# A hybrid decoder trunk on one core: the mixers' normalized input written over X, retention tables loaded once or a stage ahead, retention gates fetched ahead of the state updates

## The chip, the core and the metric

The kernel runs on one core of one Trainium2 chip. The core has TensorE (PE, with its weight loads PEld), VectorE (DVE), ScalarE (ACT), GpSimd (POOL) and SyncE (SP), each with an instruction queue of its own that it works through in order. The metric is the device time of one execution in microseconds, lower being better.

## The reference, cut to what matters

One step of a two-layer trunk over 256 prompt positions and 8 sequences of 8 sampled positions (320 columns in all). In each layer three branches read the same normalized `h`:

```python
x = x + 0.5 * swiglu_ffn(rmsnorm(x, ffn1_norm), ...)
h = rmsnorm(x, mix_norm)
q, k, v, g_ret, u, z, xbc, dt_raw, gate_logits = split(h @ w_in)
y_ret, s_ret = retention_branch(q, k, v, g_ret, ...)   # rotary; scores * decay; state update; silu(g) * groupnorm(o)
y_s5,  s_s5  = s5_branch(u, ...)
y_ssd, s_ssm = ssd_branch(z, xbc, dt_raw, ...)
x = x + (gates[0]*y_ret + gates[1]*y_s5 + gates[2]*y_ssd) @ w_out
x = x + 0.5 * swiglu_ffn(rmsnorm(x, ffn2_norm), ...)
```

In the retention branch each of the four heads multiplies its scores by a decay table of its own and the sampled queries by `q_dec`, updates its state, normalizes its output over the head and multiplies it by the gate `silu(g)`.

## The kernel before, in words

**Layout.** Activations lie transposed, 128 channels by 320 columns; X is eight such tiles. Every matrix product is made of fp32r parts: a value is split into a high half (ScalarE copy, L304) and a low half (VectorE subtraction, L305), and `proj` (L287) multiplies each 128x128 weight block three times (L294 high by high, L295 high weight by low input, L296 low weight by high input). `stream` (L267) loads 512 KB of weights at a time with SP and splits them (L280 on ScalarE, L281 on VectorE); there are three raw, two high and two low buffers. One such chunk feeds 24 matmuls, one `proj` over eight input tiles.

**The pool `t`.** All 128x320 tiles of activations and tables come from one pool of 53 (`NT`). A tile's slot is taken by the first instruction that writes it.

**Order.** The program text is not the order of the engines. `weave` (L381) deals steps of side work (state-space groups, S5 blocks, retention heads) between the units of a main list; a planner then fixes, before the run and with its own costs, the order of the instructions on each engine's queue. Slots of one pool are handed out in program order with few exceptions, so the planner places an instruction that takes a `t` tile behind the first writers of the `t` tiles asked for before it.

**Start of the mixers** (L1338 to L1359). `scaled` splits X times the norm's gain before the norm's factor r is known, and the first seven projections run on these pairs: dt (L434), three of u and three of xBC; r is multiplied in afterwards, at L436 (dt, into a new `t` tile), L1204 (u, into a new `t` tile) and L517 and L518 (xBC). `ssd_dt` first asks for a table (`resets`, L431). In `norm` (L372) each X[k] is multiplied by gain and r into a new tile h (L377) and split. All later projections read these pairs. X itself was stored to DRAM (`xd`, L418) in the FFN before and comes back only for the residual after the mixers (L1427).

**Retention.** `ret_tabs` (L790) loads the two rotary tables. Each head (`ret_head`, L864, twelve steps) issues on GpSimd the loads of its state s0 (2 x 512 KB, L870) and of two tables, its mask `mk` and `qd` (L871, issued at L208). Two steps later the scores are multiplied by the mask (L882 to L884) and the sampled queries by `qd` (L886). Keys are transposed, scaled (L894), split (L573, L574) and spread by matmuls (L583). Outputs o are made (L914 to L921), the prompt state (L928 to L931) and the eight sampled states (L936, L938) are updated and stored (L940), and then the two gate tiles are fetched from DRAM (L943, issued at L1319). There follow mean and variance (L946 to L950, the Newton steps of `rstd_of` at L338 to L347, PE's broadcast L350, ScalarE's copy L353), the product of gate, gain and o (L953), the product with r (L954) and the split. The gates were made by `ret_gate` (L958) and stored to `sd` (L967).

The heads run in two weaves (L1397, L1398), two heads in each, beside gate projections and S5 blocks. Ahead of them a weave (L1387) ends with the eight units of the last state-space projection, `o`. After the heads the first product that needs all of them is `ret_w_o` (L1406).

Of the kernel before, what the change touches and what calls it, by code (L numbers as in the profile page):

```python
# [13 lines left out]
ALU = mybir.AluOpType  # L14
# [34 lines left out]
S5P = ((0,), (1, 2), (3, 4), (5, 6), (7,))  # L49
# [106 lines left out]
class Trunk:  # L156
# [139 lines left out]
            nc.tensor.matmul(p[:, :T], wl, xh, start=False, stop=k == n - 1)  # L296
        return p

    def split(self, src, hi=None):

        nc = self.nc
        hi = self.t(F32R)
        lo = self.t(F32R)
        nc.scalar.activation(hi, src, AF.Copy)  # L304
        nc.vector.tensor_tensor(lo, src, hi.bitcast(F32), op=ALU.subtract)  # L305
        return hi, lo
# [65 lines left out]
    def norm(self, l, name, r):  # L372
        nc = self.nc
        hs = []
        for k in range(KD):
            h = self.t()
            nc.vector.scalar_tensor_tensor(h, self.X[k], self.col(l, name, k), r, op0=ALU.mult, op1=ALU.mult)  # L377
            hs.append(self.split(h))
        return hs

# [409 lines left out]
    def ret_tabs(self):  # L790
        self.rot = self.tab(0), self.tab(1)

    def ret_qk(self, l, h, rot):

        nc = self.nc
        sts = {}

        def unit(nme, hd):
            if nme not in sts:
                sts[nme] = self.stream(f"w_{nme}", l)  # L800
            cos, sin = self.rot
            p = self.proj(sts[nme], h())
            sw = self.t()
            o = self.t()
            with self.soon():
                nc.scalar.activation(sw[0:64], p[64:128, :T], AF.Copy)
                nc.scalar.activation(sw[64:128], p[0:64, :T], AF.Copy)
                nc.vector.tensor_tensor(o, p[:, :T], cos, op=ALU.mult)
            nc.vector.tensor_tensor(sw, sw, sin, op=ALU.mult)
            nc.vector.tensor_tensor(o, o, sw, op=ALU.add)  # L810
            rot[nme, hd] = o

        return [lambda n=n, hd=hd: unit(n, hd) for n in "qk" for hd in range(RH)]
# [50 lines left out]
    def ret_head(self, l, hd, rot, v, vs, sd, out):  # L864
        nc, C, ap = self.nc, self.C, self.ap
        V, S = nc.vector, nc.scalar
        kd = C["kdec"].rearrange("p (b h) -> p b h", b=3)
        s0 = [self.A(4, 256) for _ in range(2)]
        for i in range(2):
            nc.gpsimd.dma_start(out=s0[i], in_=ap["ret_in"][l][:, hd, 4 * i:4 * i + 4])  # L870
        mk, qd = self.tab(2 + hd), self.tab(6)  # L871
        yield
        yield
        q, k = rot["q", hd], rot["k", hd]
        vv, VS = v[hd // 2], vs[hd // 2]
        c8 = float(np.exp(LS * np.log1p(-np.exp2(-5.0 - hd))))
        pc = self.ps()
        nc.tensor.matmul(pc[:, 0:256], k[:, 0:128], q[:, 0:256], start=True, stop=True)
        nc.tensor.matmul(pc[:, 256:384], k[:, 128:256], q[:, 128:256], start=True, stop=True)
        nc.tensor.matmul(pc[:, 384:448], self.block(k, 2), q[:, LP:], start=True, stop=True)  # L880
        sc = self.S(448)
        V.tensor_tensor(sc[:, :256], pc[:, :256], mk[:, :256], op=ALU.mult)  # L882
        V.tensor_tensor(sc[:, 256:384], pc[:, 256:384], mk[:, :128], op=ALU.mult)
        V.tensor_tensor(sc[:, 384:], pc[:, 384:448], mk[:, LP:], op=ALU.mult)  # L884
        qp = self.pad[hd % 2]
        V.tensor_tensor(qp[:, :, :LS], q[:, LP:].rearrange("p (b t) -> p b t", b=NB),  # L886
                        qd[:, hd * NS:(hd + 1) * NS].rearrange("p (b t) -> p b t", b=NB), op=ALU.mult)
        yield
        pt = self.ps()
        for b in range(3):  # L890
            nc.tensor.transpose(pt[:, b * 128:(b + 1) * 128], self.block(k, b), C["ident"])
        kt = self.S(3, 128)
        for b in range(3):
            S.activation(kt[:, b], pt[:, b * 128:(b + 1) * 128], AF.Copy, scale=kd[:, b, hd:hd + 1])  # L894
        kh = self.stack(kt[NS:, 2], "kh")
        yield
        KT = self.tv(2, 128, dt=F32R)
        self.spread(kh, 1, KT)

        ys = []  # L900
        for hf in range(2):
            py = self.ps()
            for b in range(4):
                nc.tensor.matmul(py[32 * b:32 * b + 32, :256], qp[:, 4 * hf + b], s0[b // 2][:, 2 * (b % 2) + hf], start=True, stop=True,
                                 tile_position=(0, 32 * b))
            y = self.tv(256)
            S.activation(y, py[:, :256], AF.Copy)
            ys.append(y)
        yield
        os = []  # L910
        for e in range(2):
            vc = slice(hd % 2 * 256 + e * 128, hd % 2 * 256 + e * 128 + 128)
            po = self.ps()
            nc.tensor.matmul(po[:, 0:256], vv[:, 0, vc], sc[:, 0:256], start=True, stop=False)  # L914
            nc.tensor.matmul(po[:, 128:256], vv[:, 1, vc], sc[:, 256:384], start=False, stop=True)
            nc.tensor.matmul(po[:, 256:320], vv[:, 2, vc], sc[:, 384:], start=True, stop=False)
            for hf in range(2):
                nc.tensor.matmul(po[:, 256 + 32 * hf:288 + 32 * hf], ys[hf][:, e * 128:e * 128 + 128], C["pick"],
                                 start=False, stop=hf == 1)
            o = self.t()  # L920
            S.activation(o, po[:, :T], AF.Copy)  # L921
            os.append(o)
            yield

        vh = slice(hd % 2 * 256, hd % 2 * 256 + 256)
        pp = self.ps()
        for b in range(2):
            nc.tensor.matmul(pp[:, :256], kt[:, b], vv[:, b, vh], start=b == 0, stop=b == 1)  # L928
        rp = self.tv(256)
        S.activation(rp, pp[:, :256], AF.Copy)  # L930
        nc.gpsimd.dma_start(out=ap["ret_p"][l][:, hd], in_=rp)  # L931
        for b2 in range(NB // 2):
            pu = self.ps()
            rows = slice(32 * b2, 32 * b2 + 24)
            for hf in range(2):
                nc.tensor.matmul(pu[:, hf * 256:(hf + 1) * 256], KT[rows, hf], VS[rows, hf, vh], start=True, stop=True)  # L936
            sv = s0[b2 // 2][:, 2 * (b2 % 2):2 * (b2 % 2) + 2].rearrange("p b e -> p (b e)")
            V.scalar_tensor_tensor(sv, sv, c8, pu, op0=ALU.mult, op1=ALU.add)  # L938
            if b2 % 2:
                nc.gpsimd.dma_start(out=ap["ret_s"][l][:, hd, 4 * (b2 // 2):4 * (b2 // 2) + 4], in_=s0[b2 // 2])  # L940
                yield

        sgs = [self.fetch(sd[:, 2 * hd + e]) for e in range(2)]  # L943
        pm = self.ps()
        for e in range(2):
            nc.tensor.matmul(pm[:, :T], self.ones[256], os[e], start=e == 0, stop=e == 1)  # L946
        for e in range(2):
            V.tensor_tensor(os[e], os[e], pm[:, :T], op=ALU.subtract)
        yield
        r = self.rstd(os, 256)  # L950
        yield
        for e in range(2):
            V.scalar_tensor_tensor(os[e], sgs[e], self.col(l, "ret_ln_g", 2 * hd + e), os[e], op0=ALU.mult, op1=ALU.mult)  # L953
            V.tensor_tensor(os[e], os[e], r, op=ALU.mult)  # L954
            out.append(self.split(os[e]))
        yield
# [371 lines left out]
    def layer(self, l):  # L1328
        nc, ap = self.nc, self.ap
# [8 lines left out]
        hs, r = self.scaled(l, "mix_norm")  # L1338
# [3 lines left out]
        h = lambda: H[0]  # L1342
# [18 lines left out]
        s5 = lambda *bs: [(self.s5_block(l, Q, ud, yd, b), self.S5_STEPS) for b in bs]  # L1361
        zu = lambda g: self.ssd_gate(l, h, g, xg[g][2:], S["z"], yg[g])
# [3 lines left out]
        rot, v, vs, heads = {}, [], [], {}  # L1366
# [3 lines left out]
        sd = self.dr.tile([128, KD, T], F32, name=self.nm("sd"))  # L1370
# [6 lines left out]
        rg = self.ret_gate(l, h, S["g"], sd)  # L1377
        take = lambda n: [free.pop(0) for _ in range(n)]
# [4 lines left out]
        x, o = xu(3), ou(1)  # L1383
        self.weave(take(W4) + x[:2] + zu(1) + blend(x[2:], take(W5)) + take(W6) + o[:4] + [self.ret_tabs] + o[4:], ssd(2), s5(*S5P[0]))
        self.weave(take(W7) + qk[:2] + zu(2) + qk[2:5] + take(W8) + blend(qk[5:], ou(2)), ssd(3), s5(*S5P[1]))
        o = ou(3)
        self.weave(vu[0] + zu(3) + [vr] + vu[1] + o[:2] + [vr] + o[2:], s5(*S5P[2]))  # L1387
        yret = []
        ret = [(self.ret_head(l, hd, rot, v, vs, sd, yret), self.RET_STEPS) for hd in range(RH)]

# [3 lines left out]

        g2 = [lambda m=m: gate2(m) for m in range(KD)]
        n = len(free)
        self.weave(rg[:4] + g2[:4] + take(n // 2), ret[:2], s5(*S5P[3]))  # L1397
        self.weave(rg[4:] + g2[4:] + take(len(free)), ret[2:], s5(*S5P[4]))  # L1398
        so = self.stream("ret_w_o", l)
        ys5 = []  # L1400
# [183 lines left out]
```

## Time and profile before

| | |
|---|---|
| three runs | 2372.28, 2375.01 and 2371.87 us, median 2372.28 |
| profiled execution | 2377.88 us, of which the span from the first to the last instruction is 2376.1 us |
| mean granted clock of TensorE | 0.989 of full speed |
| busy share of the span | PE 97%, PEld 92%, DVE 74%, ACT 52%, POOL 18% |
| DMA | 455.63 MB, mean 192 GB/s |

The profiled execution is 5.6 us above the median of the three runs and 1.8 us longer than its span. A busy PE is not PE at its peak: the ends of matmuls are modelled and overlap the next start, so the pace is read from the distance of the starts. A number in brackets behind a row of a timeline is the time for which the engine sat idle before it, and what ended that.

### The profile page before, as it was taken

How to read it: one execution, taken by the hardware profiler on the slowest of the kernel's cores; microseconds unless marked ns; L12 is line 12 of the kernel's file. 1: busy time of each engine (PE TensorE's matmuls, PEld its weight loads, DVE VectorE, ACT ScalarE, POOL GpSimd, SP SyncE). 2: the span in 40 equal slices, each digit the busy share in tenths (PEclk: the TensorE clock that was granted, in tenths of full speed). 3: DMA queues.
4: the chain of work that ended last, by engine and by line, in shares of the span. 5: the costliest groups of instructions: out<-in, count | busy, mean ns of one | idle time of the engine just before them, and what ended most of it. 6: DMA issues, size and time to landing. Idle time of an engine off the chain costs nothing.

```text
span 2376.1 us, 41534 instructions
## 1 busy us (share of the span) xinstructions
PE 2294.7 (97%) x15798; PEld 2177.9 (92%) x15798; DVE 1754.0 (74%) x3398; ACT 1231.0 (52%) x2261; POOL 439.5 (18%) x858
## 2 busy tenths in 40 slices
PE   7999999999999999999999999999999999999998
PEld 7999989988898889999999999899888887999998
DVE  7989788798776556767876687888887665666554
ACT  4444477676454444444443445876574544544332
POOL 0111242221223230001000013432211232200000
PEclk9999999999999999999999999999999999999999
DMA  5767656756666565455556665766756674755553
GB/s 172 229 209 223 209 173 225 242 189 206 225 200 218 188 204 169 150 164 177 179 173 192 180 210 167 245 196 212 232 161 212 212 257 140 226 150 146 149 150 110
DMA packets 130856, 455.63 MB, mean 192 GB/s; under 512 B 19744, under 2 KB 23552, under 8 KB 130656
## 3 DMA queue, kind: packets, MB, share of 16 engines
q1 hardware_dynamic: 82080, 293.11, 40.7%
q0 software_dynamic: 48576, 159.86, 19.9%
q8 instruction: 124, 2.03, 0.3%
q14 instruction: 76, 0.62, 0.1%
HBM read 381.31 MB, written 72.89 MB: 191 GB/s over the span
## 4 chain that ended last, share of the span: by engine, by line
PE 78%; ACT 6%; DVE 6%; issue 5%; DMA 2%; POOL 2%; SPq 0%; DVEq 0%; POOLq 0%; ACTq 0%
PE pp L294 22%; PE pp L296 22%; PE pp L295 22%; DVE wlo L281 2%; ACT whi L280 2%; DMA t<-in_tabs 2%; PE pb L1238 1%; ACT B L671 1%; PE pb L350 1%; PE pb L711 1%; PE pb L718 1%; PE pb L687 1%; PE pp L836 1%; PE pp L837 1%; PE pp L838 0%
## 5 line engine op out<-in xcount | busy, mean ns | idle before, releaser
L294 PE MATMUL pp<-t,whi 128*128 128x320 f32 x4304 | 1344.2, 313 | 30.6 <-ACT t L365 12.3
L296 PE MATMUL pp<-t,wlo 128*128 128x320 f32 x4304 | 1339.5, 312 | 11.3 <-DVE wlo L281 11.1
L295 PE MATMUL pp<-t,whi 128*128 128x320 f32 x4304 | 1339.4, 312 | 0.4 <-DVE t L366 0.4
L280 ACT ACTIVATE whi<-wraw 128x1024 fp32r<-128x1024 f32 x554 | 586.2, 1059 | 779.1 <-issue 388.7
L281 DVE TENSOR_TENSOR wlo<-wraw,whi 128x1024 fp32r<-128x1024 f32 x554 | 676.7, 1222 | 265.5 <-ACT whi L280 261.9
L294 PEld LDWEIGHTS pp<-t,whi 128*128 128x128 f32 x4304 | 811.0, 189 | 49.1 <-ACT t L365 12.3
L296 PEld LDWEIGHTS pp<-t,wlo 128*128 128x128 f32 x4304 | 811.7, 189 | 25.4 <-DVE wlo L281 18.0
L295 PEld LDWEIGHTS pp<-t,whi 128*128 128x128 f32 x4304 | 812.3, 189 | 8.0 <-issue 2.6
L304 ACT ACTIVATE t<-t 128x320 fp32r<-128x320 f32 x184 | 84.3, 463 | 61.8 <-DVE t L1421 28.7
L305 DVE TENSOR_TENSOR t<-t,t 128x320 fp32r<-128x320 f32 x184 | 88.4, 486 | 18.1 <-ACT t L304 16.9
L526 DVE SCALAR_TENSOR_TENSOR acc<-xpad,cols,acc 128x344 f32<-128x344 f32 x144 | 80.0, 571 | 4.3 <-ACT acc L523 3.6
L405 DVE TENSOR_TENSOR t<-pp,t 128x320 f32<-128x320 f32 x88 | 42.7, 486 | 45.0 <-PE pp L296 39.0
L411 DVE TENSOR_TENSOR t<-t,pp 128x320 f32<-128x320 f32 x88 | 42.6, 484 | 38.6 <-PE pp L296 37.7
L671 ACT ACTIVATE B<-C,tk 128x128 f32<-128x128 f32 x192 | 63.0, 392 | 0.1
L325 ACT ACTIVATE t<-t 128x320 f32<-128x320 f32 x104 | 47.2, 460 | 25.7 <-DVE t L416 12.2
L416 DVE SCALAR_TENSOR_TENSOR t<-pp,t 128x320 f32<-128x320 f32 x64 | 31.2, 488 | 35.1 <-PE pp L296 35.0
L406 ACT ACTIVATE t<-t 128x320 f32<-128x320 f32 x88 | 40.4, 459 | 22.1 <-DVE t L405 22.0
L519 POOL COPY cso<-xpad 128x3 f32<-128x3 f32 x48 | 29.1, 607 | 104.9 <-ACT xpad L514 79.0
L1148 POOL DMA_DIRECT2D kd<-t x64 | 32.6, 516 | 78.5 <-issue 73.4
L407 DVE TENSOR_TENSOR t<-t,t 128x320 f32<-128x320 f32 x88 | 42.7, 485 | 4.5 <-ACT t L406 4.5
L1166 POOL DMA_DIRECT2D pk<-A x16 | 8.8, 552 | 188.4 <-DVE A L1164 188.4
L709 DVE TENSOR_TENSOR A<-A,dec 128x512 f32<-128x512 f32 x64 | 42.3, 685 | 1.3 <-PE pb L699 1.3
(368 smaller groups left out, 2508.8 us busy)
## 6 DMA issues: line engine op xcount, KB each, us to landing
wraw<-in_w_gu SPq DMA_DIRECT2D x176, 512.0 KB, 3.5
wraw<-in_w_down SPq DMA_DIRECT2D x88, 512.0 KB, 3.6
wraw<-in_w_xbc SPq DMA_DIRECT2D x48, 512.0 KB, 4.3
wraw<-in_w_gate SPq DMA_DIRECT2D x48, 512.0 KB, 4.6
A<-in_ssm_in POOLq DMA_DIRECT2D x32, 512.0 KB, 6.0
out_ssm_s<-A POOLq DMA_DIRECT2D x32, 512.0 KB, 5.1
wraw<-in_w_z SPq DMA_DIRECT2D x32, 512.0 KB, 4.8
wraw<-in_ssd_w_o SPq DMA_DIRECT2D x32, 512.0 KB, 3.7
```

Source lines behind the costliest of these rows:

```text
L280: nc.scalar.activation(hi[:, :w], raw[:, :w], AF.Copy)
L281: nc.vector.tensor_tensor(lo[:, :w], raw[:, :w], hi[:, :w].bitcast(F32), op=ALU.subtract)
L294: nc.tensor.matmul(p[:, :T], wh, xh, start=k == 0, stop=False)
L295: nc.tensor.matmul(p[:, :T], wh, xl, start=False, stop=False)
L296: nc.tensor.matmul(p[:, :T], wl, xh, start=False, stop=k == n - 1)
L304: nc.scalar.activation(hi, src, AF.Copy)
L305: nc.vector.tensor_tensor(lo, src, hi.bitcast(F32), op=ALU.subtract)
L325: self.nc.scalar.activation(q, x, AF.Square)
L405: V.tensor_tensor(hid[i], p[:, :T], r, op=ALU.mult)
L407: V.tensor_tensor(hid[i], hid[i], r, op=ALU.mult)
L526: nc.vector.scalar_tensor_tensor(acc[:, :n], xp[:, r:r + n], self.col(l, "conv_w", 4 * i + r), acc[:, :n], op0=ALU.mult, op1=ALU.add)
L671: S.activation(lm[:, e, o:o + 128], bc[:, i0:i0 + 128], AF.Relu, scale=-1.0, bias=tk[:, b, c:c + 1])
```

## The change

Three edits in each layer. `norm` writes h over X[k] in place of a tile of its own (X is read again only from `xd`). The mask tables and `qd` are not loaded by the heads: `qd` is loaded once per layer instead of four times, with the masks of heads 0 and 1, in a unit of its own within the weave at L1387, behind the fourth of its eight `o` units; the masks of heads 2 and 3 come in a unit at the end of the first weave of heads. The two gate fetches of a head stand ahead of its state updates in place of behind them. `split` loses a parameter that nothing uses.

```diff
     def norm(...):
         for k in range(KD):
-            h = self.t()
-            nc.vector.scalar_tensor_tensor(h, self.X[k], self.col(l, name, k), r, op0=ALU.mult, op1=ALU.mult)
+            h = self.X[k]
+            nc.vector.scalar_tensor_tensor(h, h, self.col(l, name, k), r, op0=ALU.mult, op1=ALU.mult)
             hs.append(self.split(h))
...
+    def ret_masks(self, *heads):
+        def unit():
+            if 0 in heads:
+                self.qd, self.mks = self.tab(6), {}
+            for hd in heads:
+                self.mks[hd] = self.tab(2 + hd)
+        return [unit]
...
     def ret_head(...):
-        mk, qd = self.tab(2 + hd), self.tab(6)
         yield
         yield
+        mk, qd = self.mks[hd], self.qd
...
             os.append(o)
             yield
+        sgs = [self.fetch(sd[:, 2 * hd + e]) for e in range(2)]
         (prompt state; four pairs of state updates and their stores)
-        sgs = [self.fetch(sd[:, 2 * hd + e]) for e in range(2)]
...
-        self.weave(vu[0] + zu(3) + [vr] + vu[1] + o[:2] + [vr] + o[2:], s5(*S5P[2]))
+        self.weave(vu[0] + zu(3) + [vr] + vu[1] + o[:2] + [vr] + o[2:4] + self.ret_masks(0, 1) + o[4:], s5(*S5P[2]))
...
-        self.weave(rg[:4] + g2[:4] + take(n // 2), ret[:2], s5(*S5P[3]))
+        self.weave(rg[:4] + g2[:4] + take(n // 2) + self.ret_masks(2, 3), ret[:2], s5(*S5P[3]))
```

## Rows read from the trace of the kernel before

**Rows 1.** The page, busy time and share of the span, TensorE.
```profile
PE 2294.7 (97%) x15798; PEld 2177.9 (92%) x15798; DVE 1754.0 (74%) x3398; ACT 1231.0 (52%) x2261; POOL 439.5 (18%) x858
```

**Rows 2.** Waits of PE: who was waited for, us in total, times, longest.
```profile
PE pb L583 <- DVE S L574: 9.3, 8, 2.0
PE pb L350 <- DVE rs L347: 8.5, 7, 2.3
...
PE pp L294 <- DVE t L808: 5.9, 2, 3.0
...
PE pp L294 <- DVE t L436: 2.8, 1, 2.8
```

**Rows 3.** Windows: length, busy us (instructions) by engine, PE's granted clock, DMA.
```profile
287.80:293.00 5.20, 5.04 (x24) 5.07 (x25) 3.89 (x10) 1.41 (x3) 1.63 (x5) 0.67 0.46 132
293.00:306.00 13.00, 10.43 (x54) 8.04 (x53) 9.32 (x18) 7.60 (x16) 2.86 (x6) 0.98 0.23 66
306.00:313.00 7.00, 7.00 (x40) 7.00 (x40) 4.91 (x8) 4.75 (x8) 2.19 (x5) 0.80 0.58 163
...
1470.00:1480.00 10.00, 8.85 (x57) 8.06 (x56) 8.40 (x13) 9.32 (x18) 4.48 (x9) 1.00 0.52 143
...
792.00:800.00 8.00, 7.96 (x35) 6.07 (x34) 2.69 (x7) 1.92 (x5) 2.71 (x5) 0.69 0.40 126
...
1962.00:1970.00 8.00, 7.97 (x51) 6.21 (x50) 3.68 (x7) 1.17 (x4) 4.33 (x8) 1.00 0.87 281
```

**Rows 4.** Timeline of DVE, layer 0, the norm: start, length, line, operation.
```profile
287.33 0.48 DVE L436 TENSOR_TENSOR t<-pp,t 128x320 f32<-128x320 f32 x1
...
298.81 0.55 DVE L377 SCALAR_TENSOR_TENSOR t<-t,cols,t 128x320 f32<-128x320 f32 x1
...
300.30 0.55 DVE L377 SCALAR_TENSOR_TENSOR t<-t,cols,t 128x320 f32<-128x320 f32 x1
```

**Rows 5.** Timeline of PE, layer 0, ahead of the norm.
```profile
283.83 0.31 PE L295 MATMUL pp<-t,whi 128*128 128x320 f32 x1
...
284.86 0.31 PE L296 MATMUL pp<-t,wlo 128*128 128x320 f32 x1
287.96 0.38 PE L294 MATMUL pp<-t,whi 128*128 128x320 f32 x1 [2.80 <-DVE t L436]
```

**Rows 6.** Timeline of PE, end of retention, layer 0, then layer 1.
```profile
843.19 0.31 PE L296 MATMUL pp<-t,wlo 128*128 128x320 f32 x1
845.35 0.85 PE L350 MATMUL pb<-cb,rs 128*128 128x128 f32 x6 [1.85 <-DVE rs L347]
847.76 0.63 PE L294 MATMUL pp<-t,whi 128*128 128x320 f32 x2 [1.55 <-ACT t L304]
...
2013.07 0.85 PE L350 MATMUL pb<-cb,rs 128*128 128x128 f32 x6 [2.26 <-DVE rs L347]
```

**Rows 7.** Timeline of DVE, end of retention, layer 0.
```profile
840.06 0.48 DVE L327 TENSOR_TENSOR t<-t,t 128x320 f32<-128x320 f32 x1
842.79 0.55 DVE L953 SCALAR_TENSOR_TENSOR t<-t,cols,t 128x320 f32<-128x320 f32 x1 [2.25 <-DMA t<-sd]
843.26 0.15 DVE L338 TENSOR_SCALAR rs<-pb 128x3 f32<-128x3 f32 x1
```

**Rows 8.** Timeline of POOL, end of retention, layer 0: second gate fetch of head 3.
```profile
838.14 0.54 POOL L1319 DMA_DIRECT2D t<-sd  x1
```

**Rows 9.** Line L1319, all 48 fetches: from issue to landing.
```profile
DMA to landing us min/median/max: 2.5/4.1/6.3
```

**Rows 10.** Timeline of POOL, layer 0, head 2: its two tables.
```profile
780.43 1.07 POOL L208 DMA_DIRECT2D t<-in_tabs  x2
```

**Rows 11.** Timeline of DVE, layer 0, head 2.
```profile
787.23 0.42 DVE L882 TENSOR_TENSOR S<-pb,t 128x256 f32<-128x256 f32 x1 [2.09 <-DMA t<-in_tabs]
```

**Rows 12.** Timeline of PE, layer 0, the spread of head 2, then of head 3.
```profile
788.81 0.41 PE L583 MATMUL pb<-S,exact 128*128 128x128 f32 x2 [1.97 <-DVE S L574]
...
823.82 0.44 PE L583 MATMUL pb<-S,exact 128*128 128x128 f32 x2 [1.03 <-DVE S L574]
```

More of the change, by code (lines that the diff above doesn't have):

```diff
@@ L297, in proj, with split @@
         return p
-    def split(self, src, hi=None):
+    def split(self, src):
         nc = self.nc
```

## The prediction

> **What bounds the kernel now.** I read the page first: TensorE is busy 97% of the span, 2294.7 us, and no other engine comes near it [rows 1]. So an edit can only pay where TensorE waits or runs slowly, and the next view is the list of its waits [rows 2]. The two longest that this change touches are both in the retention heads: 9.3 us in eight times for the low half of the keys (L574), and 8.5 us in seven times for the last Newton step of a group norm (L347). The list misses two things. A busy TensorE may be at half pace, so the third view is the windows with the granted clock [rows 3]. And a matmul is shown as 0.31 us long while the next starts after 0.147, so short gaps don't show; I take the pace from starts: seven steps from 283.83 to 284.86, 0.147 us each [rows 5]. From window length less matmuls times 0.147 follows what a stretch loses. Last I read the timelines of VectorE and GpSimd at those places [rows 4, 7, 8, 10, 11] for what was late there.
>
> **The norm over X.** Before, the eight steps of layer 0 run as a chain: VectorE multiplies (L377), ScalarE copies (L304), VectorE subtracts (L305), then multiplies again; the period is 300.30 - 298.81 = 1.49 us, of which 0.55 is the multiplication [rows 4]. Two projections that read the pairs as they come run beside it. The window from 293 to 306 holds 54 matmuls, worth 54 x 0.147 = 7.9 us of 13.0, so 5.1 us are lost; behind these gaps TensorE gets 0.80 of its clock for 7 us, some 2.8 of them at the lower level, 1.2 GHz in place of 2.4, which is 1.4 us more [rows 3]. In layer 1 the stretch from 1470 to 1480 holds 57 matmuls, 8.4 us of 10, and loses 1.6.
>
> Why does the chain exist and start late? r had long been there, as L436 needs it too, and TensorE stands 2.80 us for L436 [rows 5]: L436 takes a new tile of `t`, is planned behind the first writer of a tile asked for earlier (the reset table), and L377 comes behind it for the same reason. With h in X[k], L377 takes no tile any more. The planner can then place all eight when r is there, in VectorE's idle time ahead of L436. The pairs still take tiles, so L304 and L305 wait as before, but eight copies and eight subtractions can then follow each other on two engines without the multiplication between them. L436 itself doesn't move, nor do the 2.80 us. The ceiling is 5.1 + 1.4 + 1.6 = 8.1 us. I take half, 4.0, because the same stretches hold waits for weight halves (L280, L281) that needn't come from the norm. The other end: eight multiplications in one burst are 8 x 0.55 = 4.4 us of VectorE ahead of a weight half, while one chunk feeds TensorE for 24 x 0.147 = 3.5; 0.9 a layer, 1.8 us slower. The write over X waits for the store to `xd`, issued in the FFN's last units, and for the last reads by `scaled`, which r itself needs. I cost that at nothing; if the store were late, every pair would be by as much.
>
> **The tables.** Six of 22 loads go, 0.54 us of GpSimd each [rows 10], which is busy 18% [rows 1]: nothing. The others move ahead of the heads, past the state loads. In head 2 of layer 0 the tables are issued at 780.43 [rows 10] and VectorE waits 2.09 us for them, until 787.23, 6.8 us after the issue [rows 11]. The low half of the keys stands behind those products on VectorE, so TensorE's spread of the keys starts 1.97 us late [rows 12]. The edit takes this wait away. What is late next shows in head 3, whose tables were issued early: its spread still waits 1.03 us [rows 12], for the same subtraction behind S5 work. If heads 0 to 2 lost all their wait, 9.3 - 2 x 1.03 = 7.2 us would go; if all eight came down to head 3's 1.03, only 9.3 - 8 x 1.03 = 1.1 [rows 2, 12]. After that stop of 1.97 us in layer 0 the mean clock is 0.69 for 8 us, some 5 of them at 1.2 GHz, up to 2.5 us more; behind its twin in layer 1 it is 1.00, 2.4 GHz throughout [rows 3], so I don't count that. I take 3.5, a little under the middle, with 1.1 and 9.7 as bounds. The tables live longer, three more tiles at a time of 53; I see no place for a price.
>
> The Trainium skill (DMA: Bandwidth & Descriptors, Anatomy of one DMA) gives a GpSimd-issued transfer about 2.0 us plus its bytes over 436 GB/s. By that page a table of 163,840 bytes would be an estimated 2.4 us, would be there before VectorE asks, and the tables' term would be nothing: 9.0 in place of 12.5 in the sum below. The row with 6.8 us speaks against it here: two state loads of 512 KB are just ahead.
>
> **The gates.** In head 3 of layer 0 the second fetch is issued at 838.14 [rows 8], behind the stores of the states. VectorE waits 2.25 us for it at L953, and the ten Newton steps, ready but behind it, start at 843.26 although the squares were summed by 840.54 [rows 7]. TensorE stands 1.85 us at L350, and then 1.55 more for the split [rows 6]. Layer 1 has the same picture with 2.26 [rows 6]. A fetch takes 4.1 us in the median [rows 9], and VectorE could use it at 840.54, so it has to be out by 840.54 - 4.1 = 836.4, 1.7 us earlier than now; three stores of 0.54 us each alone, if each is issued like it [rows 8], are 1.6, and the four state updates that it no longer follows come on top. Late next is PE's own sum and the Newton chain, and the 1.55 us stay: nothing is ready to fill them. I take 4.0 of 1.85 + 2.26 = 4.1, and 1.0 for the heads 1, in 8.5 - 4.1 = 4.4 us that other norms share [rows 2]: 5.0. The bounds are 0 (GpSimd waits elsewhere and issues as late as before) and 8.5.
>
> **The sum.** 4.0 + 3.5 + 5.0 = 12.5 us. The profiled execution of 2377.9 would become 2365.4; the median of the three runs shown lies 5.6 lower, so 2372.3 - 12.5 = 2359.8.
>
> **Rivals.** *The norm gives nothing*: L377 is not moved or another wait replaces the chain, as L280 and L281 are next in line; the heads alone give 8.5, 2363.8. For it: TensorE is held by L436 first, which the edit leaves. Chance 0.20. *The waits move*: the tables and gates arrive early, but TensorE then waits as long for the same subtraction behind S5 work, as in head 3, and for the Newton chain; some 3 us are left, 2369. Chance 0.17. *Slower*: the fetches (eight head places) and table units (four) take `t` tiles earlier in program order. Wherever GpSimd's queue holds such a load back, first writers of later tiles are planned behind it, gate projections don't leave PSUM, and TensorE stops as at L436. One such stop costs 2.80 us [rows 5] and clock behind it, 0.67 in the mean of 1.2 and 2.4 GHz over 5.2 us, 5.2 x 0.33 = 1.7 [rows 3], 4.5 in all. It decides from four such places of twelve: 18 - 12.5, 5.5 us slower, 2377.8. For it: L808, two stops of 5.9 us together [rows 2], is of that kind. Against it: the gates were stored units earlier, and before, the heads' own table loads held tiles back in the same way. Chance 0.13. What I forecast, all three paying, has 0.50.
>
> **Numbers.** Under 0.2%, 4.7 us, counts as no change; about that can be told from it. The forecast and the first rival are faster, 0.70; 0.17 is the same; 0.13 slower. All ceilings together (8.1 + 9.7 + 8.5) would give 2346, all floors (+1.8 - 1.1) 2373. The range runs from 2350, leaving some 0.05 below, to 2373, leaving most of the slower rival above.
>
> **What would show it.** Right: L377 eight times in a row ahead of L436, L305 at a distance of about half a microsecond; no wait of L882, L886 and L953 for a DMA; PE's waits for L574 down from 9.3 to about 6, for L347 from 8.5 to about 4; clock near 1 behind head 2. Wrong: L377 still in step with L304; new stops of TensorE of 2 to 3 us at first writers of `t` (L436, L808, L1314, L966); GpSimd waiting at L1319 for a store to `sd`.

## The result and the profile after

Four executions of the changed kernel took 2340.64 to 2346.62 us, median 2344.56; four of the kernel before, measured with them, took 2371.87 to 2375.01, median 2372.91. The ratio is 0.987, 95% interval 0.9853 to 0.9886: 28.4 us or 1.3% faster. The forecast was 2359.8, with 2350 as the lower end, so the direction was right and the size less than half of what came. The profiled execution took 2343.26 us (span 2341.5, mean granted clock 0.994), 34.6 less than that of before.

The busy times of the changed kernel, from its page:

```profile
PE 2280.1 (97%) x15798; PEld 2168.7 (93%) x15798; DVE 1752.6 (75%) x3398; ACT 1231.1 (53%) x2265; POOL 435.0 (19%) x852
```

TensorE has the same 15,798 matmuls and is busy 14.6 us less [rows 1]: less busy time for equal work points to the clock (below), and to gaps too short to show. Its waits (who was waited for, us in all, times, longest; behind `ret_tabs` the lines are 9 higher than before, between the two places of the gate fetch 10):

```profile
PE pp L296 <- DVE wlo L281: 9.3, 13, 1.9
PE pp L294 <- DVE t L817: 5.9, 2, 3.0
PE pp L294 <- ACT t L304: 5.5, 3, 2.8
...
PE pb L350 <- DVE rs L347: 3.0, 5, 2.0
PE pb L1247 <- DMA t<-ud: 2.3, 1, 2.3
PE pb L583 <- DVE S L574: 2.0, 6, 0.6
```

Against [rows 2], L347 fell from 8.5 to 3.0 us and L574 from 9.3 to 2.0. L436 is off the list, and its 2.80 us stand under L304. L1247, an S5 block that waits for its input, is new. VectorE's own waits name no load of a table or a gate any more: L962, the product with the gate, has none, and the products with the tables wait for TensorE alone:

```profile
DVE S L891 <- PE pb L889: 5.1, 4, 2.2
DVE pad L895 <- PE pb L913: 1.6, 2, 0.8
```

VectorE at the norm of layer 0, as in [rows 4] (start, length, line, operation, times in a row):

```profile
271.90 2.40 DVE L377 SCALAR_TENSOR_TENSOR t<-t,cols,t 128x320 f32<-128x320 f32 x5
...
274.68 0.55 DVE L377 SCALAR_TENSOR_TENSOR t<-t,cols,t 128x320 f32<-128x320 f32 x1
...
276.30 1.00 DVE L377 SCALAR_TENSOR_TENSOR t<-t,cols,t 128x320 f32<-128x320 f32 x2
...
287.87 0.48 DVE L436 TENSOR_TENSOR t<-pp,t 128x320 f32<-128x320 f32 x1
...
289.08 3.32 DVE L305 TENSOR_TENSOR t<-t,t 128x320 fp32r<-128x320 f32 x8
```

The eight multiplications run 10 to 16 us ahead of L436, and the eight low halves follow each other at 3.32 / 8 = 0.42 us where the period was 1.49. The stop ahead of them is there still:

```profile
285.39 0.31 PE L296 MATMUL pp<-t,wlo 128*128 128x320 f32 x1
288.50 0.56 PE L294 MATMUL pp<-t,whi 128*128 128x320 f32 x1 [2.80 <-ACT t L304]
```

**Where the time came from.** As all these traces hold the same number of matmuls in nearly the same order, the start of the k-th in one can be set against the k-th in another. Time that each stretch became shorter, in us, profiled execution against profiled execution:

| stretch (matmul; us in before) | changed | norm alone | tables alone | gates alone | tables and gates |
|---|---|---|---|---|---|
| norm, layer 0 (1750 to 2000; 260 to 309) | 6.1 | 6.5 | 0.1 | 0.0 | 0.4 |
| start of ssd group 0 (to 2500; 386) | 2.8 | 2.7 | 0.0 | 0.0 | -2.3 |
| retention, layer 0 (5000 to 5750; 755 to 878) | 12.7 | -1.1 | 3.7 | 7.3 | 12.6 |
| norm and ssd group 0, layer 1 (9750 to 10500; 1452 to 1569) | 6.6 | 6.6 | 0.0 | 0.0 | 1.2 |
| retention, layer 1 (12250 to 13500; 1832 to 2024) | 5.0 | 0.4 | -2.2 | 4.7 | 4.8 |
| all, from the first matmul to the last | 34.7 | 14.4 | 5.0 | 14.8 | 19.9 |

The last four columns are the first experiments. The stretch called retention of layer 0 begins ahead of the end of head 1; that of layer 1 holds all four heads. Part of the time is clock. The same stretches as windows (length, busy us and instructions of PE, PEld, DVE, ACT and POOL, then PE's granted clock, DMA), of before:

```profile
260.20:309.00 48.80, 42.69 (x252) 39.36 (x251) 34.80 (x67) 22.54 (x39) 10.82 (x25) 0.93 0.53 159
...
755.10:877.90 122.80, 113.55 (x755) 102.97 (x752) 73.86 (x163) 55.82 (x107) 38.53 (x68) 0.96 0.62 201
1451.90:1568.50 116.60, 111.56 (x753) 103.32 (x752) 99.56 (x174) 82.96 (x171) 46.20 (x91) 0.99 0.64 202
```

and of the changed kernel:

```profile
260.30:303.00 42.70, 38.98 (x252) 37.77 (x251) 36.21 (x71) 24.29 (x43) 13.85 (x29) 0.96 0.62 183
...
747.00:857.10 110.10, 106.96 (x753) 97.68 (x752) 72.14 (x158) 53.53 (x102) 36.30 (x64) 1.00 0.68 224
1431.20:1541.10 109.90, 108.85 (x752) 102.28 (x751) 96.10 (x166) 84.07 (x172) 44.55 (x92) 1.00 0.68 215
```

Length times what the clock lacks to 1 is the time lost to the lower level: 48.8 x 0.07 = 3.4 us at the norm of layer 0 before, 42.7 x 0.04 = 1.7 after. In long stretches the two places of the clock are too coarse, so there it is added up over windows of 10 us: 5.1 us in the retention of layer 0 before, nothing after, and 25.1 against 14.3 over the span. Some 11 of the 34.6 us between these two executions are therefore clock, and some 24 are stops and gaps.

### The profile page after: what moved, and what is told of

Same layout as the page of the kernel before. It is cut to its first block, busy times and chain, and to the rows that moved or that the text cites. A ratio compares the mean times of both kernels' runs of the same rounds, so it can differ in the third digit from the quotient of the medians.

```text
span 2341.5 us, 41565 instructions
## 1 busy us (share of the span) xinstructions
PE 2280.1 (97%) x15798; PEld 2168.7 (93%) x15798; DVE 1752.6 (75%) x3398; ACT 1231.1 (53%) x2265; POOL 435.0 (19%) x852
## 3 DMA queue, kind: packets, MB, share of 16 engines
q0 software_dynamic: 48288, 158.88, 19.9%
## 4 chain that ended last, share of the span: by engine, by line
PE 85%; DVE 7%; ACT 5%; issue 2%; DMA 0%; SPq 0%; POOL 0%; DVEq 0%; ACTq 0%; POOLq 0%
PE pp L294 24%; PE pp L296 24%; PE pp L295 24%; DVE wlo L281 2%; ACT whi L280 2%; PE pb L1247 1%; PE pb L350 1%; ACT B L671 1%; PE pb L687 1%; PE pb L1295 1%; PE pb L718 1%; PE pb L711 1%; PE pb L699 1%; PE pb L335 1%; PE pp L845 1%
## 5 line engine op out<-in xcount | busy, mean ns | idle before, releaser
L280 ACT ACTIVATE whi<-wraw 128x1024 fp32r<-128x1024 f32 x554 | 586.2, 1058 | 758.8 <-issue 385.8
L281 DVE TENSOR_TENSOR wlo<-wraw,whi 128x1024 fp32r<-128x1024 f32 x554 | 676.5, 1221 | 259.6 <-ACT whi L280 257.6
L296 PEld LDWEIGHTS pp<-t,wlo 128*128 128x128 f32 x4304 | 810.2, 188 | 22.0 <-DVE wlo L281 14.4
L304 ACT ACTIVATE t<-t 128x320 fp32r<-128x320 f32 x184 | 83.5, 462 | 43.7 <-DVE t L1430 28.7
L305 DVE TENSOR_TENSOR t<-t,t 128x320 fp32r<-128x320 f32 x184 | 87.9, 485 | 13.1 <-ACT t L304 12.4
L519 POOL COPY cso<-xpad 128x3 f32<-128x3 f32 x48 | 34.1, 710 | 117.5 <-ACT xpad L514 94.9
L712 DVE TENSOR_TENSOR A<-A,pb 128x512 f32<-128x512 f32 x64 | 42.3, 679 | 1.3 <-PE pb L711 1.2
```

The source lines that it names most:

```text
L280: nc.scalar.activation(hi[:, :w], raw[:, :w], AF.Copy)
L281: nc.vector.tensor_tensor(lo[:, :w], raw[:, :w], hi[:, :w].bitcast(F32), op=ALU.subtract)
```

## The experiments

| kernel | median us | ratio to before on its chip, 95% interval |
|---|---|---|
| norm alone | 2363.36 | 0.9942 (0.9928 to 0.9955) |
| tables alone | 2372.9 | 0.9982 (0.997 to 0.9994) |
| gates alone | 2363.23 | 0.994 (0.9924 to 0.9956) |
| tables and gates | 2358.45 | 0.9919 (0.9906 to 0.9933) |
| h asked for ahead | 2376.06 | 1.0001 (0.9987 to 1.0015) |
| h in its own tiles | 2371.64 | 0.9973 (0.9958 to 0.9989) |
| resets once, before | 2358.65 | 0.9921 (0.99 to 0.9942) |
| resets once, changed | 2345.39 | 0.9867 (0.9848 to 0.9886) |
| and exponentials together | 2342.4 | 0.9849 (0.9819 to 0.9879) |
| query table by head | 2343.44 | 0.9853 (0.9822 to 0.9884) |
| projections ahead | 2356.16 | 0.9905 (0.9881 to 0.993) |
| exponentials and projections | 2352.61 | 0.9891 (0.9865 to 0.9918) |

The kernel before took 2377.01 us in the median on the chip of the first four, 2376.24 on that of the next four, 2378.29 on that of the last four.

### The three edits, one by one

**Norm alone** is the first hunk of the change on the kernel before.

```diff
-            h = self.t()
-            nc.vector.scalar_tensor_tensor(h, self.X[k], self.col(l, name, k), r, ...)
+            h = self.X[k]
+            nc.vector.scalar_tensor_tensor(h, h, self.col(l, name, k), r, ...)
```

> The kernel before with h written over X and nothing else. First theory (the norm is the larger half): the changed kernel gained 6.1 us between its 1,750th and 2,000th matmul, 3.1 at the start of ssd group 0 and 6.6 at the same two places of layer 1, all before the first head runs; if the norm does all of that, this kernel is 14 to 18 us faster than before, L377 runs ahead of L436 and the wait of L687 for L680 (2.1 us in layer 0) is gone. Rival (the forecast's size): the norm is worth 4 us, at most 8.1, and the rest comes from the heads' edits or from a new plan that any edit brings; then this kernel is 2 to 8 us faster and L687 still waits for L680.

Measured: 13.7 us faster, a little under the first theory's 14 to 18, and both of its signs are there. By the table the gain lies at the norm and the start of ssd group 0 of both layers: 6.5 + 2.7 + 6.6 = 15.8, less a little elsewhere. The pairs start little earlier than before, but follow each other without the multiplication between them. VectorE's first low half before, which the others follow at the period of 1.49 us, then all eight with the norm alone:

```profile
289.34 0.49 DVE L305 TENSOR_TENSOR t<-t,t 128x320 fp32r<-128x320 f32 x1 [0.24 <-ACT t L304]
```

```profile
288.26 3.33 DVE L305 TENSOR_TENSOR t<-t,t 128x320 fp32r<-128x320 f32 x8
```

TensorE's wait for the decays of ssd group 0 before, then its waits with the norm alone:

```profile
PE pb L687 <- DVE B L680: 6.2, 6, 2.1
```

```profile
PE pb L583 <- DVE S L574: 11.3, 10, 2.5
...
PE pb L350 <- DVE rs L347: 8.4, 7, 2.2
...
PE pb L687 <- DVE t L1262: 0.3, 2, 0.2
```

The heads wait no less than before. The wait of L687 for L680, which the prediction did not look at, is gone.

**Tables alone** and **gates alone** are the other two.

```diff
-        mk, qd = self.tab(2 + hd), self.tab(6)
         yield
         yield
+        mk, qd = self.mks[hd], self.qd
         (and ret_masks with its two places in the weaves)
```

> The kernel before with the tables loaded once a layer, a stage ahead, and nothing else; gates are fetched where they were. First theory: the stop behind L574 in head 2 of layer 0 (1.97 us) and the clock of 0.69 behind it go, L583's wait falls from 9.3 us to 4 or less, and the kernel is 5 to 9 us faster. Rival (the forecast's size): 3.5 us. Second rival: the earlier table units hold back later first writers of t and nothing is gained.

```diff
             os.append(o)
             yield
+        sgs = [self.fetch(sd[:, 2 * hd + e]) for e in range(2)]
         (prompt state; state updates and their stores)
-        sgs = [self.fetch(sd[:, 2 * hd + e]) for e in range(2)]
```

> The kernel before with the two gates of a head fetched ahead of its state updates, and nothing else. First theory: the wait of L350 for the last Newton step falls from 8.5 to about 4 us, and the kernel is 4 to 7 us faster. Rival: without the tables' edit GpSimd's queue is no earlier and under 2 us are gained.

Measured: 4.1 and 13.8 us faster. The first is under the 5 to 9 expected and nearest to the forecast's 3.5; the second is twice the 4 to 7 expected. TensorE's wait for L281 before, then its waits with the tables alone:

```profile
PE pp L296 <- DVE wlo L281: 11.1, 16, 1.9
```

```profile
PE pp L296 <- DVE wlo L281: 15.1, 18, 2.1
...
PE pb L335 <- DVE t L327: 4.4, 6, 1.7
...
PE pb L1247 <- DMA t<-ud: 1.8, 1, 1.8
PE pb L583 <- DVE S L574: 0.8, 4, 0.2
```

and with the gates alone:

```profile
PE pb L583 <- DVE S L574: 8.0, 7, 1.6
...
PE pb L350 <- DVE rs L347: 2.6, 3, 2.0
```

The tables took 8.5 us off L583, more than all the forecast's 7.2, and 7.4 came back: 4.0 at L281, 1.6 at L335 (2.8 before), 1.8 at L1247. L350 went down by 1.3. VectorE comes earlier to the gates, which are as late as ever; its wait for them (L962) grows from 7.9 us in six times to this, and the low half of a weight stands behind it, here in head 1 of layer 0 and with 2.06 us in that of layer 1 (VectorE twice, then TensorE):

```profile
DVE t L962 <- DMA t<-sd: 10.6, 7, 2.6
```

```profile
773.68 0.55 DVE L962 SCALAR_TENSOR_TENSOR t<-t,cols,t 128x320 f32<-128x320 f32 x1 [1.50 <-DMA t<-sd]
...
774.22 1.22 DVE L281 TENSOR_TENSOR wlo<-wraw,whi 128x1024 fp32r<-128x1024 f32 x1
...
775.50 0.42 PE L296 MATMUL pp<-t,wlo 128*128 128x320 f32 x1 [1.90 <-DVE wlo L281]
```

The gates took 5.9 us off L350 and 1.3 off L583. In head 3 of layer 0 the product with the gate no longer stops VectorE [rows 7]:

```profile
834.14 0.55 DVE L953 SCALAR_TENSOR_TENSOR t<-t,cols,t 128x320 f32<-128x320 f32 x1
...
836.08 0.16 DVE L338 TENSOR_SCALAR rs<-pb 128x3 f32<-128x3 f32 x1 [0.52 <-PE pb L335]
```

Clock comes on top: the retention of layer 0 loses 1.7 us to the lower level in this kernel where before lost 5.1.

**Tables and gates** is the changed kernel with h in a tile of `t` again.

> The changed kernel with h in a tile of t again: tables and gates alone. First theory: the stops of layer 0 and layer 1 from the norm to ssd group 0 are all back, and the kernel is 14 to 18 us slower than the changed one, 10 to 14 us faster than before. Rival (the forecast's size): 4 to 8 us slower than the changed one, and ssd group 0 starts without the wait of L687 for L680 here too, because the new plan removed it.

Measured: 18.6 us faster than before, and some 12 slower than the changed kernel (30.9 less 18.6), between the two theories. The wait of L687 for L680 is back in full, 6.2 us, so it was not the heads' edits that removed it. TensorE's wait for L281 is back at 11.1 us: what the tables had moved there is gone once the gates are early too, while the 1.8 us at L1247 stay. Single gains of 4.1 and 13.8 give 17.9, and with the norm's 13.7 the three give 31.6 us; the changed kernel's ratio on 2377 us is 30.9. Within the intervals the edits add up. In the two retention stretches tables and gates together took 12.6 + 4.8 = 17.4 us and by themselves 3.7 - 2.2 + 7.3 + 4.7 = 13.5; in the medians such a bonus is not shown.

### What the norm's edit is paid for

**h asked for ahead**: h stays in `t`, but its eight tiles are asked for before the pairs'.

```diff
-        hs = []
+        hs, hx = [], [self.t() for _ in range(KD)]
         for k in range(KD):
-            h = self.t()
+            h = hx[k]
```

> The kernel before, whose norm asks for its eight h tiles of t ahead of its loop, so that no pair's tiles stand between them; nothing else changes. Theory A (what the norm's edit pays for is that h leaves the order in which t is handed out): L377 still comes behind L436, in step with L304 and L305, and the kernel is within 4 us of before. Rival B (only the alternation of h, high half and low half in that order cost time): the eight multiplications follow each other and 10 us or more are gained, as with the norm alone (13.7).

**h in its own tiles**: four tiles outside `t`, which gives up three of its 53 for the room.

```diff
-NT = 53
+NT = 50
...
-            h = self.t()
+            h = self.s("nh", [128, T], bufs=4)
```

> The kernel before with h in four tiles of its own, outside t, instead of over X; t has 50 tiles in place of 53, as there is no room for both. Theory A (the order of t): the first four multiplications run ahead of L436, the other four behind a pair each; most of the gain of the norm alone, 8 to 14 us, is there without a write over X. Rival C (the gain is that t is asked for eight tiles fewer and X's tiles come free later): nothing is gained, or three tiles fewer of t cost more than that.

The first made no difference. VectorE, h asked for ahead:

```profile
286.34 0.48 DVE L436 TENSOR_TENSOR t<-pp,t 128x320 f32<-128x320 f32 x1
...
287.28 0.53 DVE L377 SCALAR_TENSOR_TENSOR t<-t,cols,t 128x320 f32<-128x320 f32 x1
...
288.35 0.49 DVE L305 TENSOR_TENSOR t<-t,t 128x320 fp32r<-128x320 f32 x1 [0.24 <-ACT t L304]
288.76 0.55 DVE L377 SCALAR_TENSOR_TENSOR t<-t,cols,t 128x320 f32<-128x320 f32 x1
```

All eight multiplications are still behind L436 and in step with the pairs. With its own tiles VectorE does four of them at 273.24, ahead of L436 at 289.21, and 4.3 us are won at the norm of layer 0 and 5.0 in layer 1. But 3.2 are given back at ssd group 0, and 4.6 us are left of the 8 to 14 expected. The order of `t` is thus what held L377, and a write over X isn't needed to leave it; that three tiles fewer cost something was not tried by itself.

**Resets once, before** takes away what L436 and L377 stand behind, without the change.

```diff
+        self.resets = self.cp.tile([128, T], F32, name="resets")
+        nc.gpsimd.dma_start(out=self.resets, in_=ap["tabs"][:, 7])    # at the start
...
-        resets = self.tab(7)
+        resets = self.resets
```

> The kernel before with the table of resets loaded once, at the start, into a tile of its own among the constants, instead of into a tile of t behind the stores to toep. Theory A (L436 and L377 stand behind that load's place in the order of t): L436 and the first L377 run when r is there, some 15 us earlier; the stop of 2.80 us and the chain behind it go from TensorE's way, ssd group 0 starts without the wait of L687 for L680 in layer 0, and 8 to 14 us are gained without the change. Rival D (L436 was held by VectorE's queue, not by the load): under 4 us.

Measured: 17.6 us, more than the 8 to 14 expected and at least as much as the norm's edit; only L687 kept 3.3 of its 6.2 us. VectorE (the third row is the last of the eight low halves):

```profile
271.29 0.48 DVE L436 TENSOR_TENSOR t<-pp,t 128x320 f32<-128x320 f32 x1
...
272.24 0.53 DVE L377 SCALAR_TENSOR_TENSOR t<-t,cols,t 128x320 f32<-128x320 f32 x1
...
290.56 0.48 DVE L305 TENSOR_TENSOR t<-t,t 128x320 fp32r<-128x320 f32 x1
```

L436 comes 16 us earlier [rows 4]. The alternation of L377, L304 and L305 is all there, spread over 18 us, and costs nothing, as it starts early enough. The stretch of the norm in layer 0 is 11.5 us shorter, and 6.0 are won at that of layer 1. (The profiled execution, 2373.33 us at a mean clock of 0.985, was the longest of this kernel's six and lost time in the heads, which the edit doesn't touch; hence the stretches, not its sum.)

### What is late next

**Resets once, changed** is the same edit on the changed kernel.

> The changed kernel with the same table loaded once, at the start. Theory A: the stop of 2.80 us that the changed kernel still has at 285 us (now L304, behind a weight half that waits for its buffer) goes, with the 1.7 us of lower clock behind it: 4 to 6 us faster than the changed kernel. Rival D: no difference of more than 2 us.

No gain: the stretch of the norm is 5.8 us shorter than in the changed kernel, and the next one 6.8 longer. ScalarE at that place, and the wait of TensorE:

```profile
312.51 1.28 ACT L529 ACT_TABLE_LOAD   x1
313.80 0.42 ACT L529 ACTIVATE t<-acc 128x256 f32<-128x256 f32 x1
...
315.41 1.28 ACT L473 ACT_TABLE_LOAD   x1
...
317.58 1.04 ACT L280 ACTIVATE whi<-wraw 128x1024 fp32r<-128x1024 f32 x1
318.64 1.28 ACT L530 ACT_TABLE_LOAD   x1
```

```profile
PE pp L294 <- ACT whi L280: 8.8, 12, 3.3
```

The dt chain (Exp) and the convolutions (Silu) meet on ScalarE here, and each turn from one to the other loads a table, five times between 308 and 325 us. The weight half L280 is behind them, and TensorE waits 3.3 us.

**Exponentials together** removes two of these turns.

```diff
-        ea = self.s("ea", [128, 1])
-        nc.scalar.activation(ea, self.col(l, "a_log", 0), AF.Exp)
+        ea = self.eas[l]                  # both layers' at the start of the kernel
...
-        nc.scalar.activation(ce, cum[...], AF.Exp)      # ahead of nrev
         nc.scalar.activation(w[:, :128], nrev[:, :128], AF.Exp, ...)
         nc.scalar.activation(w[:, 128:], nrev[:, 128:], AF.Exp, ...)
+        nc.scalar.activation(ce, cum[...], AF.Exp)
```

> The changed kernel with the resets table loaded once, as in the kernel of the run before, and two exponentials of the dt chain moved: that of a_log to the start of the kernel for both layers, that of the chunk sums behind the two others of the chain. First theory (what the resets' kernel won at 285 us it gave back at 315 us, because ScalarE loads its function table five times between 308 and 325 us, 1.28 us each, with a weight half behind it): two of these loads go, the wait of 3.3 us for that weight half shrinks to 1 us or less, and the kernel is 3 to 6 us faster than the changed one. Rival (ssd group 0 is late for another reason, and any gain ahead of it is given back there): within 2 us of the changed one.

The wait of 3.3 us is gone (L280, now L282, is down to 0.7 at the longest), but smaller ones follow in ssd group 0, and 3.7 us of that stretch stay lost. Its ratio, 0.9849, and that of the changed kernel, 0.987, have intervals that overlap: a gain over it, of which 3 to 6 us were expected, is not shown.

**Query table by head** loads `qd` for each head, a stage ahead, so that the tables are moved and not fewer.

```diff
-                self.mks[hd] = self.tab(2 + hd)
+                self.mks[hd], self.qd[hd] = self.tab(2 + hd), self.tab(6)
```

> The changed kernel with the query table loaded once for each head, as before, but a stage ahead: the tables are moved, not fewer. Theory of the prediction (the six loads saved cost nothing, the place of the others is what pays): within 2 us of the changed kernel. Rival (fewer loads and fewer tiles of t matter): 3 us or more slower, with L1247 or L891 waiting longer.

No difference from the changed kernel is shown: the profiled executions took 2343.40 and 2343.26 us. TensorE's wait for L574 is 2.0 us in both, so the place is what takes that wait away; whether the number of loads is worth the rival's 3 us is left open, as the intervals of the two ratios, 0.9853 and 0.987, are wider than that.

**Projections ahead** carries the reading of the norm to L817, where TensorE stops twice for 2.97 us; there an eviction that opens a tile of `t` comes behind the four pairs of a gate asked for before.

```diff
-        self.weave(take(W7) + qk[:2] + zu(2) + qk[2:5] + take(W8) + ...
+        self.weave(take(W7) + qk[:5] + zu(2) + take(W8) + ...
```

> The changed kernel with three projections of the queries and keys asked for ahead of the gates of ssd group 2 instead of behind them. Theory A carried to another place (an eviction that opens a tile of t stands behind the first writers of the tiles asked for earlier, here the four pairs of the gates): the two stops of 2.97 us at L817 go, and up to 3.4 us of lower clock with them: 4 to 9 us faster than the changed kernel. Rival (these stops come from ScalarE's load in that stretch): the stop comes back at the next eviction, and the kernel is within 2 us of the changed one.

Slower than the changed kernel, where 4 to 9 us of gain were expected: by about 8 us going by the ratios, 0.9905 against 0.987, whose intervals just touch; in the profiled executions the two stretches with these projections (matmuls 2,500 to 5,000 and 10,500 to 12,250) are 5.6 and 7.0 us longer. The two stops of L817 are gone, and these took their place:

```profile
PE pb L335 <- DVE t L327: 16.2, 5, 6.7
...
PE pb L350 <- DVE rs L347: 8.6, 5, 3.1
```

The projections had been the work that hid the norm of the gates. Ahead of that chain's end TensorE now stands 6.7 and 3.1 us in each layer. As the edit changes what lies around L817, it does not show whether the order of `t` or ScalarE's load made the two stops there.

**Exponentials and projections** is both edits together.

> The two previous edits of the changed kernel together (resets loaded once, exponentials moved, and the three projections asked for ahead). If both pay and at different places, their gains add up: 7 to 14 us faster than the changed kernel, some 2331 to 2338 us where that one takes 2345. If each only moves its stop on: within 3 us of it.

The 7 to 14 us did not come: by the ratios it is 5 us slower than the changed kernel, which the intervals do not tell apart. On the same chip its five executions (2350.90 to 2355.36 us) all lie above the four of the exponentials alone (2340.80 to 2345.54), as the projections' do; a gain over the projections alone, 3.6 us in the medians, is not shown. Of the kernels run, none is shown to beat the changed one.

## Why the prediction was wrong in size

**What held.** L377 ahead of L436, L305 at under half a microsecond, no waits of VectorE for tables or gates, L574 and L347 down, the clock at 1.00 behind head 2 (from 747 to 857.1 us), and 2.80 us of stop that the edit doesn't move. No new stop appeared at first writers of `t`; the rival that ends slower did not come. The chance of 0.70 stood on the right side.

**The norm, 4.0 us forecast, 13.7 measured.** The mechanism held: with the multiplication gone from between them the eight low halves come 0.42 us apart and not 1.49, and TensorE no longer waits for the chain. The step that failed is the price, "I take half, 4.0", and the ceiling of 8.1 above it. In layer 0 that ceiling, 5.1 + 1.4 = 6.5, was paid in full (6.5 in the norm alone). The waits for weight halves for which the half was taken, 1.3 us at L280 and 1.0 at L281 between 284 and 312 us, went with the chain. And the ceiling left out what stands behind the chain: the convolutions, the dt chain and the decays of ssd group 0 share VectorE with it. The dt chain's product L476, before and then in the changed kernel:

```profile
331.41 0.49 DVE L476 TENSOR_TENSOR t<-t,t 128x320 f32<-128x320 f32 x1 [0.74 <-ACT t L474]
```

```profile
318.50 0.48 DVE L476 TENSOR_TENSOR t<-t,t 128x320 f32<-128x320 f32 x1
```

It starts 12.9 us earlier where TensorE is 6 us earlier, and the decays L680 are there when L687 wants them. The stretches of ssd group 0 became 2.7 us shorter in layer 0 and, from the 10,000th matmul on, 4.1 of the 6.6 in layer 1 (1.7 of them clock); the other 2.5 stand against the forecast's 1.6. L687 had 6.2 us, the fifth of TensorE's waits, and the prediction did not follow it back. That the norm's edit removes this wait is shown by the norm alone, where it is gone, and by tables and gates, where it is back; that it does so through VectorE's queue is argued from these times. The resets loaded once add one thing: the alternation, on which the price was built, costs something only because it is late. Begun 16 us earlier it is free.

**The gates, 5.0 forecast, 13.8 measured.** The four stops of L350 in the heads went whole: 1.85 and 2.26 at the ends, 0.93 and 0.84 in heads 1, 5.9 in all where the sum had 5.0. The two in heads 1, of before:

```profile
775.37 0.88 PE L350 MATMUL pb<-cb,rs 128*128 128x128 f32 x6 [0.93 <-DVE rs L347]
...
1945.17 0.88 PE L350 MATMUL pb<-cb,rs 128*128 128x128 f32 x6 [0.84 <-DVE rs L347]
```

The step that failed is that the sum stopped there. L583 lost 1.3 us (head 2 of layer 0 fell from 1.97 to 1.42, the two heads 0 by 0.7 together; by what way is not shown), and the clock gave back 5.1 - 1.7 = 3.4 us in the retention of layer 0. Clock had been counted for the norm, left out for the tables as it showed in one layer only, and not asked after for the gates; even the bound of 8.5 was the sum of waits. With 5.9 + 1.3 + 3.4 and 0.9 less at L280 the sum is 11.5, and the two retention stretches of the gates alone became 7.3 + 4.7 = 12.0 shorter. The rest of the 13.8 lies outside them and is not accounted for.

**The tables, 3.5 forecast, 4.1 measured**: the size is luck, as it came about in another way than the one given. What was late next was not "the same subtraction behind S5 work", whose 1.03 us in head 3 fell to 0.20. It was the gates, for the 4.0 of the 7.4 us that came back at L281. The rival in which the waits move was right of the tables alone, though not of where they went, and wrong of the three together. The Trainium skill (DMA: Bandwidth & Descriptors, Anatomy of one DMA), by whose figures a table would be there in an estimated 2.4 us and the edit worth nothing, does not agree with the runs: the loads of tables took 3.7 to 7.1 us to land in the kernel before, median 5.5, and 3.0 to 5.6 in the changed one, median 4.3, and the edit alone was worth 0.06 to 0.3%.

**The base.** The sum was made against one execution. Between the profiled executions the difference is 34.6 us, between the medians 28.4; the last section shows how far executions of before lie apart.

## What to carry to other kernels

Where slots of a pool are handed out in program order, ask of a late instruction which first writer it stands behind, and follow everything that stands behind it, to the next stage's longest wait; breaking the order at either end paid (the tile that isn't taken 13.7 us, the load that isn't late 17.6), and asking in another order within it paid nothing. Price a stop of TensorE with the time at the lower clock behind it, and give no edit a ceiling from the wait list alone. An edit that brings work forward is worth what the next late thing leaves of it, so look for what it uncovers (the gates behind the tables, ScalarE's table loads behind the resets), and don't take away the work that covers a chain.

## What the runs showed of the hardware

**The spread goes with the clock.** Twenty-three executions of the kernel before on one chip took from 2369.46 us (mean granted clock 0.993) to 2385.11 (0.986): 15.7 us apart, and 0.007 of 2380 us is 16.7. The work and its order are the same in each. What makes the clock differ from one execution to the next is not shown. The spread of the changed kernel is 6.0 us over four executions, of the same with the resets loaded once 1.2 over five and with the query table by head 8.6 over five; so few do not show whether the removal of stops makes it smaller.

**ScalarE's table loads.** Each change between Exp and Silu showed as 1.28 us, with 0.01 to 0.03 us between it and a neighbour that had nothing else to wait for (312.51 + 1.28 = 313.79, and L529 starts at 313.80; 317.58 + 1.04 = 318.62, and the load for L530 starts at 318.64). The Trainium skill (ScalarE: Activation LUTs, What ACT_TABLE_LOAD costs) states the same 1283 ns and 1380 ns of drain more; these rows show no such drain.
